# The low part of a group's first masked tile on GpSimd in layer 1's attention

## The chip, the cores and the metric

One core of one Trainium2 chip runs the kernel. The metric is the device time of one execution in microseconds; the number that counts is the median of the runs. The engines are TensorE (PE, with its weight loads as PEld), VectorE (DVE), ScalarE (ACT), GpSimd (POOL) and SyncE (SP), which issues the DMAs.

## The reference

Two layers of a backbone over 256 context tokens and 2048 latent tokens, 1024 wide. Layer 0 is latent attention beside a pooling branch. Layer 1, where the change lies, is windowed attention with grouped queries: 16 heads of 64, four groups of four heads that share a key head, blocks of 128 tokens, each reading its own block, its two neighbours within 128 tokens, and 256 cached context tokens, with a sink logit for each head.

```python
s_loc = jnp.einsum('bnqkgd,bnskd->bnkgqs', qb, kw).astype(jnp.float32) * scale
rel = kpos[:, None, :] - qpos[:, :, None]
valid = (jnp.abs(rel) <= SWA_WINDOW) & (kpos[:, None, :] >= 0) & (kpos[:, None, :] < T)
s_loc = jnp.where(valid[None, :, None, None], s_loc, NEG_INF)
s_ctx = jnp.einsum('bnqkgd,bpkd->bnkgqp', qb, ck).astype(jnp.float32) * scale
p = jax.nn.softmax(jnp.concatenate([s_loc, s_ctx, sk], axis=-1), axis=-1)
o = jnp.einsum('bnkgqs,bnskd->bnqkgd', p_loc, vw) + jnp.einsum('bnkgqp,bpkd->bnqkgd', p_ctx, cv)
```

A left neighbour's keys are masked along one diagonal and a right neighbour's along the other; the own block and the context are not masked.

## The kernel before

Everything is float32, and each product is made of high and low parts: a number is split into a part that PE reads in its short format (`fp32r`) and the rest. For a tile of probabilities that means the exponential (`pf`), its high part (`ph`) and the low part `pl = pf - ph`.

Layer 1's attention goes through 18 units of 128 queries (`UN1`, lines 1054 to 1058): two for the context tokens with two tiles of keys, and 16 for the latent ones. Each unit has four groups of heads (`g`), and each group goes through its tiles `i` of 128 keys by 4 x 128 queries. A unit inside has five: 0 the left neighbour (masked), 1 the own block, 2 the right neighbour (masked), 3 and 4 the context. The first latent unit has no left neighbour and the last no right one, so 15 units x 4 groups have a masked tile 0. In all there are 328 tiles (`seq1`).

Step `k` of the loop (lines 1288 to 1302) issues `scores1` of tile k, `low1` of tile k - 1, some look-ahead work (`approx1`: rough scores and their maximum, reduced by DVE in lines 1109 and 1115), and `pv1` of tile k - 3.

- `scores1`: two matmuls into one of three `S` banks (lines 1170, 1171). An unmasked tile gets its high part from ACT (line 1174). The exponential itself (line 1176) goes to one of two `bpf` buffers where the tile is masked or its low part is made by POOL, and back into its PSUM bank otherwise. A masked tile is then cut by POOL (line 1180).
- `low1`: a masked tile gets its high part now, by a copy on ACT, or on DVE in the last three units (line 1186). The low part is line 1188; `y1` says which engine makes it: POOL for tiles 1 and 3, DVE for the others.
- `pv1`: three matmuls into the bank `A` or `B` (lines 1200 to 1202); the third, line 1202, reads the low part. After the last tile of a group the sums are copied out and stored.

Every second unit `recip1` reads row sums back by DMA and adds them on DVE (line 1217). The output's weights and its first block of inputs (`mix_part`, lines 847, 848) are prepared in the same stretch. Instructions carry the waits that their tiles and buffers need. The order on each engine is not the code's: a planner (line 1409, `schedule_with_timeline_sim`) lays the program out by a clock of its own, puts on each engine what is ready by that clock, earlier code first, and hands out buffers as they come free by it.

Of the kernel before, what the change touches and what calls it, by code (L numbers as in the profile page):

```python
# [8 lines left out]
F32 = mybir.dt.float32  # L9
# [3 lines left out]
ALU = mybir.AluOpType  # L13
# [25 lines left out]
def hybrid_step(ctx: ExitStack, tc: tile.TileContext, I, O):  # L39
    nc = tc.nc  # L40
    pe, act, dve, pool, sp = nc.tensor, nc.scalar, nc.vector, nc.gpsimd, nc.sync

    def open_pool(name, side="left"):
        st = ExitStack()
        p = st.enter_context(tc.tile_pool(name=name, bufs=1, side=side, reuse_waits="tile"))
        return p, st.close
# [5 lines left out]
    def f(ap):  # L52
        return ap.bitcast(F32)
# [5 lines left out]
    def bank(tag, bufs):  # L59
        return psum.tile([128, 512], F32, tag=tag, name=tag, bufs=bufs)  # L60
# [988 lines left out]
    def key(kt):  # L1049
        if kt in (16, 17):  # L1050
            return ring["KAC"], ring["KBC"], VAC, VLC, kt - 16
        return KAR, KBR, VAR, ring["VLR"], kt - 12 if kt > 17 else kt % 8

    UN1 = [(128 * i, [(18, None), (19, None)]) for i in range(2)]
# [102 lines left out]

    LAG1, LATE = 3, NU1 - 3

    def y1(g, i):  # L1160
        return i in (1, 3)

    def scores1(u, g, i):
        bt = box["bt"]
        kt, mk = UN1[u][1][i]
        ka, kb, va, vl, t = key(kt)
        c = slice(128 * t, 128 * t + 128)
        qa, qb = [q[:, 4 * g:4 * g + 4] for q in QV[u % NQ]]
        S = bank("S", 3)
        pe.matmul(S, lhsT=ka[:, g, c], rhs=qa, start=True, stop=False)  # L1170
        pe.matmul(S, lhsT=kb[:, g, c], rhs=qb, start=False, stop=True)  # L1171
        ph = bt.tile([128, 512], F32R, tag="bph", name="bph", bufs=6)
        if mk is None:
            act.activation(out=ph, in_=S, func=AF.Exp, scale=SWA_SCALE)
        pf = S if mk is None and not y1(g, i) else bt.tile([128, 512], F32, tag="bpf", name="bpf", bufs=2)
        act.activation(out=pf, in_=S, func=AF.Exp, scale=SWA_SCALE)  # L1176
        if mk is not None:
            s = 1 - 2 * mk
            p4 = pf.rearrange("p (h n) -> p h n", h=4)
            pool.affine_select(out=p4, in_=p4, pattern=[[0, 4], [-s, 128]], base=0, channel_multiplier=s, compare_op=ALU.is_ge, fill=0.0)  # L1180
        live1[u, g, i] = (ph, pf)

    def low1(u, g, i):
        ph, pf = live1[u, g, i]
        if UN1[u][1][i][1] is not None:
            (dve.tensor_copy if u >= LATE else act.copy)(ph, pf)
        pl = box["bt"].tile([128, 512], F32R, tag="bpl", name="bpl", bufs=5)
        (pool if y1(g, i) else dve).tensor_tensor(out=pl, in0=pf, in1=f(ph), op=ALU.subtract)  # L1188
        live1[u, g, i] = (ph, pl)

    def pv1(u, g, i):
# [67 lines left out]
    bt, close_bt = open_pool("bt")  # L1259
# [28 lines left out]
    for k in range(-22, NST1 + LAG1 + 8):  # L1288
        now1[0] = k
        for fn in events1.pop(k, []):  # L1290
            fn()
        want = int(np.interp(k, *pace))
        q1_to(min(want // 8 + 2, sdone1[0] + NQ))
        if 0 <= k < NST1:
            scores1(*seq1[k])
            if k + 1 == NST1 or seq1[k + 1][0] != seq1[k][0]:
                sdone1[0] += 1
        if 1 <= k <= NST1:
            low1(*seq1[k - 1])
        look1_to(want)  # L1300
        if LAG1 <= k < NST1 + LAG1:
            pv1(*seq1[k - LAG1])
# [110 lines left out]
```

## Time and profile before

| what | us |
|---|---|
| median of three runs (lowest, highest) | 3175.36 (3166.04, 3183.04) |
| the profiled execution, its own time | 3180.69 |
| its span, first to last instruction | 3179.0 |
| layer 1's attention within the span | 2434 to 2945 |

In the page a busy share is that of the whole span, and a line number can be a helper's. The idle time that stands behind a group is put down to what ended it. Matmuls overlap: their shown length is longer than the step from one to the next. The times in the sections below are from the profiled execution.

### The profile page before, as it was taken

The numbers are of one execution on the slowest core, as the hardware profiler recorded it, in microseconds if no ns is written. First come the engines' busy times: TensorE is split into PE (matmuls) and PEld (weight loads), VectorE is DVE, ScalarE is ACT, GpSimd is POOL, SyncE is SP. The second block draws the span as 40 slices with busy tenths as digits, with TensorE's granted clock in tenths as the row PEclk, the third lists the DMA queues.
The fourth block names the chain that finished last, engine by engine and source line by source line (L and its number), as shares of the span: only waits on it lengthen the run. The fifth ranks groups of instructions, "written<-read, shape, count | busy, mean of one in ns | idle before, by whom it ended". The sixth has DMA issues, their size and how long they took to land.

```text
span 3179.0 us, 53411 instructions
## 1 busy us (share of the span) xinstructions
PE 3022.1 (95%) x19192; PEld 2596.5 (82%) x19192; DVE 2270.6 (71%) x4123; ACT 1776.8 (56%) x3579; POOL 1588.1 (50%) x1430
## 2 busy tenths in 40 slices
PE   6999998999999999999999999999997999999998
PEld 4999987897777777767789999999995776666997
DVE  6656757878898898888857556666325788787555
ACT  6444444436777777777774432323324777775432
POOL 3223242206877777877875435555001554545453
PEclk8999999999999999999999999999998999999999
DMA  6444468743202211221125463347436445541553
GB/s 237 146 142 140 143 203 251 236 129 89 55 18 57 61 45 31 52 73 37 54 64 176 153 198 126 120 127 209 131 103 132 87 101 102 112 88 47 164 172 113
DMA packets 380006, 375.31 MB, mean 118 GB/s; under 512 B 27796, under 2 KB 345276, under 8 KB 378588
## 3 DMA queue, kind: packets, MB, share of 16 engines
q1 hardware_dynamic: 379716, 371.90, 41.7%
q8 instruction: 150, 2.46, 0.3%
q14 instruction: 116, 0.95, 0.1%
q10 hardware_dynamic: 24, 0.01, 0.0%
HBM read 242.13 MB, written 129.24 MB: 117 GB/s over the span
## 4 chain that ended last, share of the span: by engine, by line
PE 59%; DVE 15%; DMA 11%; issue 5%; POOL 4%; ACT 4%; SPq 1%; DVEq 0%; POOLq 0%; ACTq 0%
PE S L113 9%; PE S L114 9%; PE S L115 9%; PE B L642 4%; PE M L553 4%; PE A L639 4%; PE M L114 3%; PE M L115 3%; PE M L113 3%; DVE pm L554 2%; PE S L1171 1%; PE S L1170 1%; DMA stg<-in_ada_w 1%; DVE xb L200 1%; DMA q_d<-ehl 1%
## 5 line engine op out<-in xcount | busy, mean ns | idle before, releaser
L629 POOL TENSOR_TENSOR acc<-acc,ph 128x512 f32<-128x512 f32 x352 | 459.6, 1306 | 58.6 <-ACT ph L605 43.8
L605 ACT ACTIVATE ph<-S 128x512 fp32r<-128x512 f32 (+1 forms) x592 | 350.4, 592 | 190.4 <-PE S L115 180.9
L554 DVE TENSOR_REDUCE pm<-M 128x1 f32<-128x512 f32 (+1 forms) x656 | 390.7, 625 | 36.3 <-PE M L553 32.8
L617 DVE TENSOR_TENSOR pl<-S,ph 128x512 fp32r<-128x512 f32 (+1 forms) x496 | 332.6, 676 | 65.7 <-ACT S L610 59.3
L113 PE MATMUL S<-hh,wh 128*128 128x256 f32 x1296 | 370.7, 287 | 5.8 <-ACT hh L199 3.0
L114 PE MATMUL S<-hl,wh 128*128 128x256 f32 x1296 | 369.6, 285 | 3.7 <-DVE hl L201 3.7
L115 PE MATMUL S<-hh,wl 128*128 128x256 f32 x1296 | 369.5, 285 | 2.5 <-POOL wl L57 2.5
L610 ACT ACTIVATE S<-S 128x512 f32<-128x512 f32 (+1 forms) x496 | 292.0, 589 | 0.0
L113 PEld LDWEIGHTS S<-hh,wh 128*128 128x128 f32 x1296 | 250.0, 193 | 10.0 <-ACT wh L56 3.3
L114 PEld LDWEIGHTS S<-hl,wh 128*128 128x128 f32 x1296 | 250.4, 193 | 6.0 <-DVE hl L201 4.3
L115 PEld LDWEIGHTS S<-hh,wl 128*128 128x128 f32 x1296 | 250.2, 193 | 4.3 <-POOL wl L57 2.9
L113 PE MATMUL S<-QS,KHL 97*128 97x512 f32 (+1 forms) x592 | 235.1, 397 | 2.5 <-DVE pl L617 2.0
L114 PE MATMUL S<-QS,KHL 97*128 97x512 f32 (+1 forms) x592 | 232.9, 393 | 0.0
L642 PE MATMUL B<-pl,VV 128*65 128x512 f32 (+1 forms) x592 | 230.6, 395 | 2.3 <-DVE pl L617 1.6
L115 PE MATMUL S<-QS,KHL 97*128 97x512 f32 (+1 forms) x592 | 232.0, 392 | 0.0
L553 PE MATMUL M<-KHL,QS 96*128 96x512 f32 (+1 forms) x656 | 219.5, 380 | 5.6 <-DVE pm L554 5.3
L639 PE MATMUL A<-ph,VV 128*128 128x512 f32 (+1 forms) x592 | 208.9, 396 | 0.7 <-ACT ph L605 0.7
L1188 POOL TENSOR_TENSOR bpl<-bpf,bph 128x512 fp32r<-128x512 f32 x136 | 178.3, 1311 | 58.8 <-ACT bpf L1176 42.9
L113 PE MATMUL M<-hh,oh 128*128 128x256 f32 x696 | 198.3, 285 | 4.0 <-ACT oh L56 4.0
L114 PE MATMUL M<-hl,oh 128*128 128x256 f32 x696 | 196.5, 282 | 0.0
L115 PE MATMUL M<-hh,ol 128*128 128x256 f32 x696 | 196.3, 282 | 0.0
L1180 POOL TENSOR_SCALAR_AFFINE_SELECT bpf<-bpf 128x512 f32<-128x512 f32 x120 | 77.1, 642 | 210.2 <-ACT bpf L1176 197.1
(387 smaller groups left out, 9636.6 us busy)
## 6 DMA issues: line engine op xcount, KB each, us to landing
q_d<-ehl SPq DMA_DIRECT2D x126, 256.0 KB
stg<-in_ada_w SPq DMA_DIRECT2D x48, 512.0 KB
xb<-in_xT SPq DMA_DIRECT2D x18, 1024.0 KB
xb<-x_d SPq DMA_DIRECT2D x18, 1024.0 KB
stg<-in_w SPq DMA_DIRECT2D x35, 512.0 KB
hh<-q_d SPq DMA_DIRECT2D x24, 512.0 KB
kn_d<-ehl SPq DMA_DIRECT2D x40, 256.0 KB
v_d<-ve SPq DMA_DIRECT2D x20, 512.0 KB
```

The costliest lines, as they stand in the source:

```text
L113: pe.matmul(ps, lhsT=wh, rhs=xh, start=i == 0, stop=False)
L114: pe.matmul(ps, lhsT=wh, rhs=xl, start=False, stop=False)
L115: pe.matmul(ps, lhsT=wl, rhs=xh, start=False, stop=i == n - 1)
L553: pe.matmul(ps[:, :w], lhsT=QS[u % 4][0:96, 0, 128 * s:128 * s + 128], rhs=KH[h % 2][0:96, c0:c0 + w], start=True, stop=True)
L554: dve.tensor_reduce(out=pms[u][:, s, i:i + 1], in_=ps[:, :w], axis=AX.X, op=ALU.max)
L605: act.activation(out=ph[:, :n], in_=S[:, :n], func=AF.Exp, scale=MLA_SCALE)
L610: act.activation(out=pf[:, :n], in_=S[:, :n], func=AF.Exp, scale=MLA_SCALE)
L617: (pool if i in YS else dve).tensor_tensor(out=pl[:, :n], in0=pf[:, :n], in1=f(ph)[:, :n], op=ALU.subtract)
L629: pool.tensor_tensor(out=acc[:, :n], in0=acc[:, :n] if ph0 is None else f(ph0)[:, :n], in1=f(ph)[:, :n], op=ALU.add)
L639: pe.matmul(A[:, :n], lhsT=V[:, kts[i], 0:128], rhs=ph[:, :n], start=i == 0, stop=i == nk - 1)
L642: pe.matmul(B[0:65, :n], lhsT=V[:, kts[i], 64:129], rhs=pl[:, :n], start=i == 0, stop=i == nk - 1)
L1188: (pool if y1(g, i) else dve).tensor_tensor(out=pl, in0=pf, in1=f(ph), op=ALU.subtract)
```

## The change

`y1` gets the unit in place of the group and is true for tile 0 too where that tile is masked. So in 60 groups (units 3 to 17, four groups each) the subtraction of tile 0 is issued to POOL, not DVE. `scores1` asks `y1` as well, but a masked tile had a `bpf` buffer already. Everything else stands.

```diff
-    def y1(g, i):
-        return i in (1, 3)
+    def y1(u, i):
+        return i in (1, 3) or i == 0 and UN1[u][1][0][1] is not None
...
-        pf = S if mk is None and not y1(g, i) else bt.tile([128, 512], F32, tag="bpf", name="bpf", bufs=2)
+        pf = S if mk is None and not y1(u, i) else bt.tile([128, 512], F32, tag="bpf", name="bpf", bufs=2)
...
-        (pool if y1(g, i) else dve).tensor_tensor(out=pl, in0=pf, in1=f(ph), op=ALU.subtract)
+        (pool if y1(u, i) else dve).tensor_tensor(out=pl, in0=pf, in1=f(ph), op=ALU.subtract)
```

## Rows read from the trace of the kernel before

**Rows 1.** The page's part 4: the chain that ended last, share of the span.

```profile
PE 59%; DVE 15%; DMA 11%; issue 5%; POOL 4%; ACT 4%; SPq 1%; DVEq 0%; POOLq 0%; ACTq 0%
```

**Rows 2.** Windows, layer 1's attention: length, then PE, PEld, DVE, ACT, POOL busy.

```profile
2434.00:2945.00 511.00, 478.69 (x2258) 340.86 (x2256) 401.10 (x920) 361.72 (x705) 252.89 (x257) 0.98 0.44 91
```

**Rows 3.** Waits, 2477 to 2942 us: who waited for whom, total us, times, longest.

```profile
ACT bpf L1176 <- DVE bpl L1188: 35.9, 36, 3.8
...
PEld A L1202 <- DVE bpl L1188: 14.5, 16, 3.9
...
PEld B L1202 <- DVE bpl L1188: 11.3, 16, 1.3
...
PE A L1202 <- DVE bpl L1188: 7.2, 8, 3.5
...
PE B L1202 <- DVE bpl L1188: 4.3, 8, 0.8
...
ACT bpf L1176 <- POOL bpl L1188: 3.4, 2, 3.0
```

**Rows 4.** Groups, 2434 to 2945 us: count, busy us, mean ns, idle before and releasers.

```profile
L1188 DVE TENSOR_TENSOR bpl<-bpf,bph 128x512 fp32r<-128x512 f32 x116 | 113.5, 978 | 16.9 <-ACT bph L1186 15.4
...
L1188 POOL TENSOR_TENSOR bpl<-bpf,bph 128x512 fp32r<-128x512 f32 x130 | 170.6, 1313 | 42.6 <-ACT bpf L1176 35.4 <-PE S L1171 2.9 <-ACT bph L1186 2.4
L1180 POOL TENSOR_SCALAR_AFFINE_SELECT bpf<-bpf 128x512 f32<-128x512 f32 x120 | 77.1, 642 | 210.2 <-ACT bpf L1176 197.1 <-PE M L1106 4.8 <-PE A L1201 3.0
```

**Rows 5.** Line 1188's DVE instructions: shortest, median, longest in ns, first and last start.

```profile
L1188 DVE TENSOR_TENSOR bpl<-bpf,bph x116: 675/742/1773, 2482.2 to 2936.8; 128x512 fp32r<-128x512 f32 x116
L1188 DVE TENSOR_TENSOR bpl<-S,bph x76: 628/680/692, 2409.1 to 2938.4; 128x512 fp32r<-128x512 f32 x76
```

**Rows 6.** Timeline of one group, engine by engine: start, length, idle before it.

```profile
2679.24 0.60 ACT L1176 ACTIVATE bpf<-S 128x512 f32<-128x512 f32 x1
...
2681.87 0.60 ACT L1176 ACTIVATE bpf<-S 128x512 f32<-128x512 f32 x1 [1.52 <-DVE bpl L1188]
...
2683.32 0.60 ACT L1176 ACTIVATE bpf<-S 128x512 f32<-128x512 f32 x1
2683.80 0.63 ACT L1186 CAST bph<-bpf 128x512 fp32r<-128x512 f32 x1
...
2680.38 1.40 DVE L1188 TENSOR_TENSOR bpl<-bpf,bph 128x512 fp32r<-128x512 f32 x1
...
2684.46 1.38 DVE L1188 TENSOR_TENSOR bpl<-bpf,bph 128x512 fp32r<-128x512 f32 x1 [0.95 <-ACT bph L1186]
...
2679.93 1.30 POOL L1188 TENSOR_TENSOR bpl<-bpf,bph 128x512 fp32r<-128x512 f32 x1 [0.35 <-ACT bpf L1176]
2682.55 0.64 POOL L1180 TENSOR_SCALAR_AFFINE_SELECT bpf<-bpf 128x512 f32<-128x512 f32 x1 [1.31 <-ACT bpf L1176]
2684.00 1.29 POOL L1188 TENSOR_TENSOR bpl<-bpf,bph 128x512 fp32r<-128x512 f32 x1 [0.82 <-ACT bpf L1176]
...
2682.74 0.39 PE L1202 MATMUL A<-bpl,VAR 128*65 128x512 f32 x1
2682.96 0.39 PE L1200 MATMUL A<-bph,VAR 128*65 128x512 f32 x1
...
2685.42 0.40 PE L1201 MATMUL A<-bph,VLR 128*64 128x512 f32 x1
2685.89 0.45 PE L1202 MATMUL A<-bpl,VAR 128*65 128x512 f32 x1
```

**Rows 7.** Timeline of DVE from 2516 us: a wait of `recip1` and what follows.

```profile
2519.13 0.19 DVE L1217 TENSOR_TENSOR rsum<-rsum 128x32 f32<-128x32 f32 x1 [2.87 <-DMA rsum<-o_d]
...
2521.60 0.69 DVE L1188 TENSOR_TENSOR bpl<-bpf,bph 128x512 fp32r<-128x512 f32 x1
```

**Rows 8.** Timeline of POOL and PE around the longest wait for a low part.

```profile
2773.11 2.50 POOL L847 TENSOR_TENSOR mg<-mg,mr 128x512 f32<-128x512 f32 x2 [2.24 <-issue]
...
2777.89 0.69 PE L1202 MATMUL A<-bpl,VAR 128*65 128x512 f32 x1 [3.49 <-DVE bpl L1188]
```

## The prediction

> **What bounds the kernel now.** I read the chain, the busy times of a stretch, the waits, and then groups and timelines of single places. The page's chain first: what ended last runs 59% through TensorE (PE) and 15% through VectorE (DVE) [rows 1]. Then the stretch of layer 1's attention, the only one that the change touches: 2434 to 2945 us, 511 us, with PE busy 478.7, DVE 401.1, ScalarE (ACT) 361.7 and GpSimd (POOL) 252.9 [rows 2]. So PE bounds it, and whatever the change does to DVE or POOL reaches the end only through PE's waits. These are 511 - 478.7 = 32.3 us of shown idle in all.
>
> The waits tell which of it has to do with the low parts. PE sat idle for a DVE low part (`bpl`, line 1188) for 7.2 + 4.3 = 11.5 us; its weight loader, which runs ahead of it, for 14.5 + 11.3 = 25.8 us in 32 waits [rows 3]. A 512-column matmul is shown 0.39 us long, but where nothing waits the next one starts 0.22 to 0.24 us after it [rows 6], so up to 0.16 us of each wait is drawn as busy: 11.5 + 32 x 0.16 = 16.6 us. That is the most that the change can give through these waits, 0.5% of the span. Put beside the loop's order (328 matmuls of line 1202, one a tile), the waits over 0.06 us are 11 before a group's first tile, 8.5 us together, with 3.5 of it in one [rows 8], and 17 before the third tile, 7.7 us, of which rows 6 end with one.
>
> **Why a third tile waits.** The masked and the POOL-made tiles of a group share two `bpf` buffers. In the group of [rows 6] exp of tile 1 ends at 2679.84; POOL makes its low part from 2679.93 to 2681.23; DVE starts tile 0's low part at 2680.38 and ends at 2681.78, 0.55 after POOL; 0.09 later ACT begins tile 2's exp, which had waited 1.52 us for that buffer. The same happens with tiles 3 and 2 (POOL 2684.00 to 2685.29, DVE to 2685.84), and PE's matmul stands at 2685.89 for it. ACT waits for a DVE low part 35.9 us in 36 waits, for a POOL one only 3.4 us in 2 [rows 3].
>
> DVE is slow here because it is held: its low parts out of SBUF take 675 ns at least, 742 in the middle and 1773 at most, those that read one operand from PSUM 680 in the middle and never over 692 [rows 5]. In rows 6 each held one ends just after POOL's. The Trainium skill says so as a rule (SBUF — State Buffer, Who interferes with whom): a VectorE instruction with two SBUF inputs and a GpSimd one that reads SBUF exclude each other, and the later one blocks fully. The trace agrees, by the 0.55 us between the two ends; a sum by the rule is the one that follows.
>
> **The change, part by part.**
> 1. Removed from DVE: 60 low parts (15 units x 4 groups whose first tile is masked). The 116 out of SBUF are these 60 and the 56 third tiles, mean 978 ns [rows 4]: 60 x 0.978 = 58.7 us of DVE's 401, of which 60 x (0.978 - 0.680) = 17.9 us is being held. DVE is not the bound; by itself this gives PE nothing, except where a first tile stood behind something else on DVE. Such a place: at 2519.13 DVE had idled 2.87 us for the DMA of `recip1`, and a first tile's low part was made only at 2521.60 [rows 7].
> 2. Added to POOL: 60 x 1.313 = 78.8 us [rows 4]. POOL goes from 252.9 to 331.7 of 511 us, 65%: not a bound by its sum. It idles 210 us before the masks, nearly all of it for ACT [rows 4]. No DMA is issued by the moved step, and no queue of SP is passed.
> 3. The order on POOL. The code issues tile 0's low part before tile 1's, but tile 1 is ready first: its exp ends at 2679.84, while the copy that tile 0's low part needs follows that exp on ACT, as the copy of tile 2 follows tile 3's exp at 2683.80 [rows 6]. The planner puts ready work first: POOL's mask of tile 2 is issued before tile 1's low part in the code and runs after it in rows 6. So: mask 0, low 1, low 0, mask 2, low 3. Low 0 then ends at 2681.23 + 1.29 = 2682.52, not 2681.78: 0.74 us later.
> 4. What that does to PE. The matmul of low 0 stood at 2682.74 [rows 6], so here it still finds it ready. Where it stood right behind DVE's end it is 0.7 us later. I count four first tiles whose matmul already waited by over 0.3 us with POOL's tile 1 just ahead (units 4, 8, 10, 12): 4 x 0.74 = 3.0 us lost, and in the last two units, where PE has no look-ahead matmuls to fill with, some 2 us more.
> 5. What it does to the buffers. The planner gives a buffer to the first tile that needs one after it came free; that low 1 can be that one is seen in the two waits of ACT for POOL [rows 3]. Now it is always low 1, free at 2681.23. Tile 2's exp starts at 2681.28, not 2681.87; mask 2 waits for low 0 until 2682.52, as it stood before (2682.55); tile 3's exp takes the other buffer at 2682.8, not 2683.32; low 3 runs 2683.45 to 2684.75, not 2684.00 to 2685.29; low 2 on DVE, held as now, ends at 2685.30, not 2685.84; and the matmul that stood at 2685.89 (0.47 us after its neighbour, so 0.24 late) finds it. The next group may start half a microsecond sooner, against waits of 0.1 to 1 us. Of the third tiles' 7.7 us I take 6 as gone.
> 6. First tiles' own 8.5 us. In the 3.5 us one POOL itself was late: two multiplications of 2.50 us for the output's first block stood ahead of tile 1's low part [rows 8]. That one stays. Of the other 5.0 some 2 stand in the groups of point 4; the 3 behind other DVE work I take as gone, and 2 us more in places like rows 7, where the look-ahead's reductions stood in the same queue.
>
> Behind the moved step on POOL stand mask 2 and low 3; for them wait ACT's copy (DVE's in the last three units), DVE's low 2 and PE's matmul: point 5 has their times.
>
> Sum: -6 - 3 - 2 + 3 + 2 = -6 us. Bounds: all of the waits gone, -16.6; nothing gone and the losses of 4 doubled, +10. What is late next: DVE's low part of tile 2, still held by POOL, and PE itself.
>
> The profiled execution took 3180.69 us, a span of 3179.0 and 1.7 around it; -6 on it is 3174.7. The median of the runs is 3175.36 (3166.04 to 3183.04), and the forecast is for a median: 3175.4 - 6 = 3169 us.
>
> **The rivals.**
> A. *No net change*, 3175 us. PE is 94% busy in the stretch; what the third tiles win the first ones lose. The Trainium skill has a sentence for it (Perfetto Trace Analysis, Optimizing Scalar/DVE Operations): the two engines share a read port, so moving work between them "might not help". Rows 5 speak for it, the 0.74 us against 0.59 us in the group above too; against it that PE has its slack at the first tile.
> B. *Slower, by POOL's queue.* It decides at which buffer the planner gives tile 2. If that stays tile 0's, or if low 0 goes ahead of low 1 and the planner holds the rest behind it, tile 2's exp starts at 2682.57, 0.7 us later than before, mask 2 and low 3 behind it, and PE, with 0.38 us between the third tile's low part and its matmul on the mean of the 56, loses about 0.74 - 0.38 = 0.36 us in each of 56 groups: +20 us, 3195 us. For it: six steps in a row on one engine. Against it: the two waits for POOL in rows 3, and that tile 1 is ready first in nearly all groups.
> C. *Much faster.* All 16.6 us of waits go, and with DVE freed its look-ahead reductions come sooner: 3158 us.
> D. *It doesn't reach the chip as written.* The planner moves other work by its own clock; a first tile whose mask came early might leave the order untouched and DVE's freed time be spent waiting. In time this is A.
>
> **How the numbers follow.** Forecast 0.48, A with D 0.32, B 0.10, C 0.10. A measurement of this kernel tells about 0.5% (16 us) from no change. Faster by more needs nearly all of C, or the forecast with 10 us more: 0.10. Slower by more is most of B: 0.08. Same: 0.82. The range takes in the forecast, A, the bounds -16.6 and +10, and leaves out most of B: 3156 to 3186 us.
>
> **What would show it.** On POOL 196 low parts of about 1.3 us, 60 more; on DVE 56 out of SBUF, still held, 76 out of PSUM unchanged at 680 ns. ACT's wait for a DVE low part falls from 35.9 us to below 12, and one for POOL's rises. PE's waits for DVE's low parts fall by half or more, and new ones for POOL's come, of 3 to 6 us. The forecast is wrong if ACT's tile 2 waits for tile 0's low part (B), if PE's waits for POOL's low parts are over 10 us (A or B), or if the stretch outside layer 1's attention moves by more than a few microseconds.

## The result, and the profile after

The changed kernel takes 3268.0 us (median; 3267.23 to 3271.03) against 3176.02 before in the same comparison (3166.04 to 3183.04): a ratio of 1.0286, with an interval of 1.0269 to 1.0303. It is 92 us slower; the forecast was 3169 us in a range of 3156 to 3186. The profiled execution took 3267.23 us with a span of 3265.5, so 86.5 us of span are to be found.

First the place. Windows of units 3 to 15, from the first score matmul of unit 3 to that of unit 16: length, then busy time of PE, PEld, DVE, ACT and POOL with instructions, mean granted clock of PE, share and rate of the DMAs. The kernel before:

```profile
2477.50:2883.60 406.10, 389.93 (x1841) 279.33 (x1840) 338.20 (x795) 305.77 (x595) 206.00 (x213) 0.99 0.47 96
```

The kernel after, the same 13 units, then the rest of the attention:

```profile
2482.20:2976.60 494.40, 422.71 (x1861) 290.72 (x1860) 299.85 (x746) 315.95 (x599) 273.67 (x266) 0.93 0.39 79
2976.60:3034.60 58.00, 54.28 (x261) 37.48 (x260) 28.69 (x41) 33.25 (x62) 43.04 (x40) 1.00 0.20 55
```

494.4 - 406.1 = 88.3 us: the whole loss lies in these 13 units, in which the change lies too. It is not in DVE (38 us less busy) nor in POOL (busy 55% of the stretch). PE's idle time, by length less busy, rose from 16.2 to 71.7 us, and its mean granted clock fell from 0.99 to 0.93. As the clock has two levels here, 0.50 and 1.00, a mean of 0.93 says that 0.07 x 2 of 494.4 us, some 69 us, went by at the lower one (1.2 GHz), against some 8 us before.

The waits name what PE stood for (2480 to 3035 us: who waited for whom, total us, times, longest); the rows answer to [rows 3]:

```profile
POOL bpl L1188 <- ACT bph L1186: 46.1, 48, 2.4
...
ACT bpf L1176 <- POOL bpl L1188: 31.9, 52, 3.1
...
PE M L1106 <- DMA hh<-q_d: 27.2, 7, 5.2
...
PE M L1106 <- DMA mix0h<-q_d: 14.8, 4, 5.1
...
ACT bpf L1176 <- DVE bpl L1188: 11.7, 14, 2.2
...
PE M L1132 <- DVE bmm L1125: 8.3, 11, 1.1
...
PE A L1202 <- DVE bpl L1188: 5.0, 8, 2.2
PE B L1202 <- POOL bpl L1188: 4.8, 8, 0.7
PE A L1200 <- ACT bph L1186: 4.8, 3, 3.8
...
PE B L1202 <- DVE bpl L1188: 3.7, 5, 0.9
...
PE A L1202 <- POOL bpl L1188: 1.6, 3, 0.7
...
PE B L1200 <- ACT bph L1186: 1.3, 5, 0.3
```

The low parts are a small matter: 8.7 us for DVE's and 6.4 for POOL's, 15.1 together against 11.5 before [rows 3]. The large rows are lines that the change does not touch: the look-ahead's first matmuls (line 1106) stand for the DMA of their queries (`hh` and `mix0h`, read from `q_d`), 42.0 us in 11 waits, one in each of units 5 to 15. The kernel before has one such wait, in unit 15:

```profile
PE M L1106 <- DMA hh<-q_d: 2.1, 1, 2.1
```

This is one of the 11, in unit 8 (timeline, SP's DMA issues and PE; start, length, idle before):

```profile
2659.81 0.60 SPq L1084 DMA_DIRECT2D mix0h<-q_d  x1
...
2661.14 0.58 SPq L1085 DMA_DIRECT2D mix0h<-q_d  x1
...
2664.21 0.39 PE L1201 MATMUL B<-bph,VLC 128*64 128x512 f32 x1
2668.19 1.19 PE L1106 MATMUL M<-KAR,mix0h 128*128 128x128 f32 x4 [3.59 <-DMA mix0h<-q_d]
...
2670.46 0.63 PE L1201 MATMUL B<-bph,VLC 128*64 128x512 f32 x1
2670.88 0.63 PE L1170 MATMUL S<-hh,KAR 128*128 128x512 f32 x1
2671.31 0.63 PE L1171 MATMUL S<-hl,KBR 96*128 96x512 f32 x1
...
2677.61 0.40 PE L1200 MATMUL A<-bph,VAR 128*65 128x512 f32 x1
2677.85 0.40 PE L1201 MATMUL A<-bph,VLR 128*64 128x512 f32 x1
```

and the windows of the wait, of the time behind it and of the time after that:

```profile
2664.50:2668.20 3.70, 0.11 (x2) 0.04 (x1) 0.00 (x0) 0.92 (x2) 2.97 (x3) 0.78 1.22 212
2668.20:2673.00 4.80, 4.80 (x14) 3.73 (x15) 1.65 (x5) 0.58 (x1) 0.04 (x1) 0.50 0.33 48
2673.50:2678.00 4.50, 4.50 (x28) 3.77 (x27) 3.52 (x12) 3.36 (x7) 1.89 (x2) 1.00 0.18 41
```

The load of unit 10's queries is issued at unit 8's start, because the three buffers of queries are used in turn and this one came free only with unit 7's last scores (unit 10 takes unit 7's buffer). The look-ahead on these queries is the next thing in PE's order; it starts 7.05 us after the second DMA's issue, having waited 3.59. Then 512-column matmuls start every 0.43 us at a granted clock of 0.50, and from 2673.5 on every 0.23 to 0.24. In the kernel before, at the start of its unit 9, such a load is issued and first read so:

```profile
2659.88 0.59 SPq L1084 DMA_DIRECT2D hh<-q_d  x1
2660.51 0.67 SPq L1085 DMA_DIRECT2D hh<-q_d  x1
...
2672.07 0.45 PE L1106 MATMUL M<-KAR,hh 128*128 128x384 f32 x1
```

There is other work in between, and nothing waits.

What moved is therefore PE's order, which the planner writes. I count by how much the look-ahead is ahead: the units of it that stand before a unit's first score matmul on PE, less the units already scored (the **lead**; 1.0 means that the unit about to start has its maxima and no more, 2.0 that the next one has them too). Before, it is 1.12 at unit 3, 1.38 to 1.88 at units 4 to 14, and 2.0 first at unit 15, the one unit with a wait for queries. After, it is 1.12 at unit 3, 1.5 at unit 4 and 2.0 from unit 5 on, where the waits begin. 2.0 is the point at which the next look-ahead needs the queries whose load has only just become possible.

The balance for units 3 to 15, with the waits taken from this stretch alone: 42.0 - 2.1 = 40 us of waits for queries; 2 us more for low parts (11.9 against 9.5 before), 8 for the maxima (8.3 against 0.5), 6 for ACT's copies of line 1186 (4.8 + 1.3, none before). Then the half clock. Part of its 69 us went by within the waits, where nothing is lost: the granted clock is 0.78 in the window of the wait above and 0.67 to 0.87 in seven of the 11, some 13 us at the lower level in all. That leaves 69 - 13 - 8 = 48 us more of work at half speed than before, some 24 us lost. Together 80 of 88.3 us; the other 8 are not accounted for (PE has 20 matmuls more in this stretch, 1861 against 1841).

### The profile page after: what moved, and what is told of

It reads as the page before. It is cut to its first block, busy times and chain, and to the rows that moved or that the text cites. A ratio compares the mean times of both kernels' runs of the same rounds, so it can differ in the third digit from the quotient of the medians.

```text
span 3265.5 us, 53434 instructions
## 1 busy us (share of the span) xinstructions
PE 3057.1 (94%) x19192; PEld 2606.2 (80%) x19192; DVE 2228.2 (68%) x4063; ACT 1788.3 (55%) x3579; POOL 1667.7 (51%) x1490
## 4 chain that ended last, share of the span: by engine, by line
PE 58%; DVE 15%; DMA 12%; issue 5%; POOL 5%; ACT 4%; SPq 1%; DVEq 0%; POOLq 0%; ACTq 0%
PE S L114 8%; PE S L113 8%; PE S L115 8%; PE M L553 3%; PE B L642 3%; PE A L639 3%; PE M L114 3%; PE M L115 3%; PE M L113 3%; DMA hh<-q_d 2%; DVE pm L554 2%; PE S L1170 1%; DVE pl L617 1%; PE S L1171 1%; DVE xb L200 1%
## 5 line engine op out<-in xcount | busy, mean ns | idle before, releaser
L1188 POOL TENSOR_TENSOR bpl<-bpf,bph 128x512 fp32r<-128x512 f32 x196 | 251.8, 1298 | 93.3 <-ACT bph L1186 48.4
L1109 DVE CUSTOM_DVE_ANT_0 junk<-M,band 128x384 bf16<-128x384 f32 (+1 forms) x256 | 132.5, 535 | 110.2 <-PE M L1106 107.8
```

The lines of the kernel that those rows point to most:

```text
L1188: (pool if y1(u, i) else dve).tensor_tensor(out=pl, in0=pf, in1=f(ph), op=ALU.subtract)
```

## The experiments

Two theories go through the expectations. **T1**: the loss is the look-ahead's place in PE's order (each wait for the queries, and the half clock behind it); the 60 moved low parts cost or give next to nothing by themselves. **T2**: the loss is the moved work itself, six steps in a row on POOL for each group (rival B of the prediction), and the look-ahead only drifts because of it. A kernel whose name begins with a is the changed one with an edit, with b the one before with the same edit. Ratios are against the kernel before, run beside each.

**The edge.** The first edit makes the look-ahead's instructions wait, in the planner's order, for the last score matmul issued ahead of them in the code. The lead is then 1.0 in both kernels:

```diff
-            approx1(u, g, hp)
+            if box.get("last") is None:
+                approx1(u, g, hp)
+            else:
+                with tc.issue_after(box["last"]):
+                    approx1(u, g, hp)
...
-        pe.matmul(S, lhsT=kb[:, g, c], rhs=qb, start=False, stop=True)
+        box["last"] = pe.matmul(S, lhsT=kb[:, g, c], rhs=qb, start=False, stop=True).ins
```

`a_pin`, the changed kernel with the edge:

> The changed kernel, with one edge more: on TensorE each look-ahead step is queued behind the second score matmul that the code issues just before it, so the planner can't pull it forward; in the built order the look-ahead then stands 1.0 units ahead throughout (2.0 in the changed kernel, 1.1 to 1.9 in the kernel before). Theory 1 (the look-ahead was pulled forward until it stood right behind the load of its queries; TensorE waits for that DMA once a unit, and its clock falls after): no more waits of over 2 us for that load, 3165 to 3190 us. Theory 2 (GpSimd's longer chain itself costs 1.5 us for each of the 60 moved tiles): 3240 to 3270 us.

Measured: 3258.4 us, 1.0244 (1.0215 to 1.0272).

`b_pin`, the kernel before with the edge:

> The kernel before with the same edge, as a control: what the edge itself does. Both theories: 3165 to 3190 us; a difference between this and the changed kernel with the edge is what the moved low parts cost or give when the order of the look-ahead is the same.

Measured: 3285.7 us, 1.0324 (1.0292 to 1.0355). T1's numbers for both were missed: the waits for queries are gone, but another took their place. At a lead of 1.0 a unit's maxima are ready only as it starts, and they have to go through a DMA (`bms`, line 1135) into the rows that the second score matmul reads. In `b_pin` (line numbers 4 higher), around unit 9's start:

```profile
2711.61 0.25 ACT L1134 COPY bms<-M 32x128 f32<-32x128 f32 x1
...
2713.74 1.86 SPq L1135 DMA_DIRECT2D hl<-bms  x1
...
2722.12 0.76 PE L1175 MATMUL S<-hl,KBR 96*128 96x512 f32 x1 [5.92 <-DMA hl<-bms]
```

and its sums of waits:

```profile
PE S L1175 <- DMA hl<-bms: 44.8, 9, 6.3
PE S L1175 <- DMA mix0l<-bms: 17.2, 5, 5.6
```

In `a_pin` the two rows say 28.6 us in 9 and 7.9 in 3. So the look-ahead has a late input on either side: too early and it stands for its queries, too late and the scores stand for its result. Both give one wait of 2 to 6 us in most units, and most such units take 34 to 40 us, where before most take 29 to 33. T2 is hurt too: with the same edge the kernel with the moved low parts is the faster one, by 27 us. At this lead the moved work is not without worth, then: the maxima are what is late, and they come sooner. From the end of a unit's last look-ahead matmul (line 1114) to the issue of its maxima's DMA went 5.1 to 6.8 us in `a_pin` and 7.0 to 7.9 us in `b_pin`, with 11.2 once (units 4 to 16), and the waits for `bms` are 36.5 us against 62.0. Which of the steps between, on DVE, ACT and SP, gave this was not tested.

`a_u6`, only the 16 low parts of units 3 to 6 moved:

```diff
-        return i in (1, 3) or i == 0 and UN1[u][1][0][1] is not None
+        return i in (1, 3) or i == 0 and u < 7 and UN1[u][1][0][1] is not None
```

> Only the first 16 of the 60 tiles are moved (units 3 to 6), the rest stays on VectorE. In the built order the look-ahead still climbs to 2.0 units ahead at unit 5 and stays there to the end. Theory 1: nearly the whole loss stays, 3235 to 3270 us, with a wait for the queries in each unit to 15, though those units are as before. Theory 2: 16 x 1.5 = 24 us, about 3200 us.

Measured: 3227.7 us, 1.0139 (1.0105 to 1.0173), between the two. Units 3 to 6 took 140.6 us (122.0 before); units 8 to 15, in which nothing is moved, took 273.6 (254.9 before). In those the lead stayed at 2.0 and PE waited once a unit, in all but unit 11, for `q_d`, 0.9 to 3.3 us. So 19 us of loss stand in units with the work as before, which T2 can't give; that the waits are shorter there, T1 as I had put it does not say.

`a_bpf3`, the change with a third `bpf` buffer:

```diff
-        pf = S if mk is None and not y1(u, i) else bt.tile([128, 512], F32, tag="bpf", name="bpf", bufs=2)
+        pf = S if mk is None and not y1(u, i) else bt.tile([128, 512], F32, tag="bpf", name="bpf", bufs=3)
```

> The changed kernel with three buffers for the exponentials (bpf) in place of two. In the built order the look-ahead stands 1.1 to 1.5 units ahead. Theory 1: 3160 to 3185 us, no wait of over 2 us for the queries. Theory 2: the chain on GpSimd is as long, though a third buffer relieves it: 3200 to 3260 us.

Measured: 3181.2 us, 1.0002 (0.9988 to 1.0016). The whole loss is gone. With the third buffer the planner wrote an order with a lead of 1.12 to 1.5 (units 3 to 15), no wait of PE for `q_d` is left, and the clock is at its upper level nearly throughout (units 3 to 15):

```profile
2483.70:2880.10 396.40, 384.07 (x1819) 275.20 (x1818) 305.64 (x715) 300.56 (x593) 270.15 (x264) 1.00 0.49 98
```

These are 9.7 us less than in the kernel before, which units 16 and the time ahead of unit 3 use up again (38.8 us for unit 16 against 34.7, and unit 3 starts 6.2 later). This run alone doesn't tell T1 from T2, since the buffer takes away the waits on POOL as well as changing the order.

**The same order in both kernels.** To take the planner out, a second edge, beside the first, makes each score matmul wait for the look-ahead's last matmul issued ahead of it, so that scores and look-ahead stand on PE in the code's order; the number of steps by which the code issues the look-ahead ahead sets the lead (8, 15 and 20 below):

```diff
-            pe.matmul(ps[:, 256 * i:256 * i + 256], lhsT=qa[:, h0 + i], rhs=ka, start=i == 0, stop=i == 1)
+            box["ahead"] = pe.matmul(ps[:, 256 * i:256 * i + 256], lhsT=qa[:, h0 + i], rhs=ka, start=i == 0, stop=i == 1).ins
...
-        want = int(np.interp(k, *pace))
+        want = min(int(np.interp(k + 8, *pace)), 8 * (sdone1[0] + NQ))
...
-            scores1(*seq1[k])
+            with tc.issue_after(box["ahead"]):
+                scores1(*seq1[k])
```

`a_mid2`, the changed kernel, 8 steps, lead 1.5:

> As a_mid1, and the scores can't pass the look-ahead either: both stand on TensorE in the code's order, 1.5 units ahead. It has b_mid2 as its partner, with the same order of scores and look-ahead and the 60 tiles on VectorE. Theory 1: within 1% of b_mid2, either way, both under 3215 us. Theory 2: 60 to 90 us above b_mid2.

Measured: 3217.2 us, 1.013 (1.0108 to 1.0153).

`b_mid2`, the kernel before, 8 steps, lead 1.5:

> The kernel before with the order of a_mid2, 1.5 units ahead. Theory 1: 3170 to 3215 us, with no wait of over 2 us once a unit. Theory 2: the same.

Measured: 3221.5 us, 1.0134 (1.0108 to 1.0161). Both lie a little over the 3215 us that T1 set as their limit. A fixed order costs both some 40 to 44 us, so it is no remedy; but within it, with the scores and the look-ahead in the same order on PE, the 60 moved low parts are worth -4 us, with intervals of 7 us either way: nothing that can be told. What the change was meant to touch did move, ACT's wait for a DVE low part (line 1180 here), in `b_mid2` and then in `a_mid2`:

```profile
ACT bpf L1180 <- DVE bpl L1192: 70.8, 62, 3.1
...
ACT bpf L1180 <- DVE bpl L1192: 5.5, 7, 1.6
```

The time shows nothing of it.

`b_lead`, the kernel before, 15 steps, lead 1.88:

> The kernel before, no tile moved, with both orders fixed as in b_mid2 and the pace 15 steps earlier in place of 8: the look-ahead stands 1.9 units ahead, just behind the load of its queries, nearly as in the changed kernel. Theory 1: the loss comes without any moved tile: a wait of 3 to 5 us for the queries in each unit from 3 to 15 and half the clock behind it, 50 to 90 us above b_mid2. Theory 2: as b_mid2 within 15 us.

Measured: 3222.3 us, 1.0144 (1.0121 to 1.0166); the loss that T1 foretold did not come. In this order the look-ahead on new queries begins some 8 us into a unit. Unit 8:

```profile
2660.12 0.60 SPq L1084 DMA_DIRECT2D mix0h<-q_d  x1
2660.78 0.66 SPq L1085 DMA_DIRECT2D mix0h<-q_d  x1
...
2668.60 0.47 PE L1106 MATMUL M<-KAR,mix0h 128*128 128x128 f32 x2
```

7.82 us after the second issue nothing is left to wait for. The lead as such costs nothing; what T1 needs is that PE comes to the look-ahead before the queries have landed, in the 7 to 8 us behind the second issue.

`b_lead20`, the kernel before, 20 steps, lead 2.0:

> The kernel before, no tile moved, both orders fixed as in b_mid2 and b_lead, the pace 20 steps earlier: the look-ahead of a unit now begins at the very step at which its queries are loaded, 2.0 units ahead as in the changed kernel. In b_lead (1.9) it began 8 us later and no wait for the queries came. Theory 1, sharpened (what costs is a first user right behind its DMA, not the lead as such): a wait of 2.5 to 5 us for the queries in each unit and 3 to 7 us of half clock behind it, 40 to 80 us above b_mid2's 3221. Rival (the wait and the clock are hidden by other work, and the moved tiles make the loss): within 15 us of b_mid2.

Measured: 3290.3 us, 1.0353 (1.033 to 1.0375), 69 us over `b_mid2` with no low part moved. Its waits are those of the changed kernel:

```profile
PE M L1106 <- DMA hh<-q_d: 24.6, 8, 4.3
PE M L1106 <- DMA mix0h<-q_d: 13.7, 4, 4.3
```

and so are its clock and its time in the window of units 3 to 15:

```profile
2498.00:2994.60 496.60, 431.26 (x1814) 292.98 (x1813) 349.74 (x756) 306.64 (x593) 206.84 (x213) 0.92 0.39 78
```

`b_mid2`, the same window:

```profile
2488.70:2922.50 433.80, 394.10 (x1814) 268.56 (x1813) 338.07 (x756) 303.37 (x593) 209.30 (x213) 0.99 0.44 90
```

The same number of instructions on every engine, and 62.8 us more in these 13 units; PE's idle time differs by 25.6 us, and the clock of 0.92 against 0.99 stands for the rest. This shows T1's mechanism without the change.

**Other leads.** Three more kernels have the first edge alone with an earlier look-ahead.

`a_mid1`, the changed kernel, 8 steps, lead 1.5:

> The changed kernel with the edge of a_pin (look-ahead not ahead of the code's scores) and the pace 8 steps earlier: in the built order the look-ahead stands 1.5 units ahead, between a_pin's 1.0, where the scores waited for the DMA of the maxima, and the changed kernel's 2.0, where the look-ahead waits for the queries. Theory 1 (a DMA that lands just behind its first user, once a unit, and the clock after it, make the loss; the moved tiles themselves cost next to nothing): no such wait on either side, 3165 to 3190 us. Theory 2 (the moved tiles cost 1.5 us each in whatever order): over 3240 us.

Measured: 3202.5 us, 1.0067 (1.0039 to 1.0094). In units 3 to 15 PE waits neither for `q_d` nor for `bms`, as T1 said, but the time is 12 us over its range; `b_mid1`, next, comes out alike without the moved work, so it is put down to the edge and the pace.

`b_mid1`, the kernel before with the same edit; its lead came out at 1.0 to 1.5 (with one wait of 3.0 us for `bms` left):

> The kernel before with the edge and the pace of a_mid1: its partner, no tile moved. In the built order the planner puts the look-ahead 1.0 to 1.5 units ahead, not 1.5 throughout. Theory 1: 3175 to 3215 us, within 1% of a_mid1 (3203).

Measured: 3197.5 us, 1.0064 (1.0044 to 1.0084). Five microseconds apart, within their intervals, though the two orders are alike and not the same: again the moved low parts are worth nothing that can be told.

`a_p12`, the changed kernel, 12 steps, lead 1.75:

> As a_mid1 (1.5 units ahead, 3203 us) with the pace 12 steps earlier in place of 8: 1.75 units ahead, as the kernel before has it in its middle, with all 60 tiles moved. Theory 1, sharpened: still no wait for the queries of over 1 us in most units, 3185 to 3215 us; the loss comes only at 2.0. Rival (the loss grows with the lead): some 3235 us, halfway to the changed kernel.

Measured: 3200.9 us, 1.007 (1.0051 to 1.0089). From the changed kernel's 3268.0 an edge that only holds the look-ahead back to a lead of 1.5 or 1.75 takes off 66 us; neither has a wait for `q_d`.

`b_bpf3`, the kernel before with three `bpf` buffers:

> The kernel before with three bpf buffers: the partner of a_bpf3 (3181 us), no tile moved. In the built order the look-ahead stands 1.0 to 1.1 units ahead. If the moved tiles cost or give little by themselves: 3165 to 3200 us. If 1.0 is too late for the maxima's DMA as in a_pin, up to 3260 us with waits for that DMA.

Measured: 3211.0 us, 1.0092 (1.0067 to 1.0117): a buffer more makes it slower. The planner wrote an order with a lead of 1.0 and 1.12 in turn, and the waits are those of `b_pin`, in six units:

```profile
PE S L1171 <- DMA hl<-bms: 18.4, 4, 4.9
PE S L1171 <- DMA mix0l<-bms: 8.8, 2, 4.5
```

So an edit that removes waits lost 1% by the order it brought about, as the change itself did; and of the 30 us between `a_bpf3` and `b_bpf3` these waits are 27, while `a_bpf3` has none for `bms` in units 3 to 15. Their orders differ, so the pair does not say what the low parts are worth.

No kernel here was faster than the one before by more than its interval.

## Why the prediction was wrong

It forecast 3169 us; the time was 3268.0. By its own steps:

- **1 and 2, the moved work: right.** POOL has 196 low parts, 251.8 us in all, 1298 ns each (1313 was taken); DVE keeps 56 out of SBUF and 76 out of PSUM at 683 ns. The rows of line 1188 after, against [rows 5]:

```profile
L1188 POOL TENSOR_TENSOR bpl<-bpf,bph x196: 1259/1288/1767, 2413.5 to 3029.9; 128x512 fp32r<-128x512 f32 x196
...
L1188 DVE TENSOR_TENSOR bpl<-S,bph x76: 627/683/692, 2414.7 to 3028.4; 128x512 fp32r<-128x512 f32 x76
L1188 DVE TENSOR_TENSOR bpl<-bpf,bph x56: 677/687/1758, 2491.0 to 3008.8; 128x512 fp32r<-128x512 f32 x56
```

- **The hold on DVE: right.** In the next fence DVE's low part starts 0.56 us after POOL's, takes 1.28 us and ends 0.55 after it, the same 0.55 as before [rows 6]. The rule of the Trainium skill that the prediction named for it (SBUF — State Buffer, Who interferes with whom) agrees with this row too.

- **3, the order on POOL: wrong.** It was to be mask 0, low 1, low 0, mask 2, low 3. A group at 2699 us, after:

```profile
2700.14 1.29 POOL L1188 TENSOR_TENSOR bpl<-bpf,bph 128x512 fp32r<-128x512 f32 x1
2700.70 1.28 DVE L1188 TENSOR_TENSOR bpl<-bpf,bph 128x512 fp32r<-128x512 f32 x1 [5.89 <-ACT bph L1186]
...
2702.06 1.08 ACT L1176 ACTIVATE bpf<-S 128x512 f32<-128x512 f32 x2
...
2702.72 0.63 POOL L1180 TENSOR_SCALAR_AFFINE_SELECT bpf<-bpf 128x512 f32<-128x512 f32 x1 [1.29 <-ACT bpf L1176]
2703.39 0.62 ACT L1186 CAST bph<-bpf 128x512 fp32r<-128x512 f32 x1 [0.25 <-POOL bpf L1180]
2704.09 2.48 POOL L1188 TENSOR_TENSOR bpl<-bpf,bph 128x512 fp32r<-128x512 f32 x2 [0.73 <-ACT bph L1186]
```

  The exponentials of tiles 0 and 1 end at 2703.14. After the mask of tile 0 POOL could make low 1, but it stands 0.73 us for ACT's copy and then makes low 0 and low 1 one behind the other; 48 such waits make 46.1 us. Low 0 goes first, as in the code. The step took "ready first by the trace" for "first by the planner's clock", and these are two clocks.

- **4 to 6, the waits for low parts: half right.** ACT's wait for a DVE low part fell from 35.9 to 11.7 us (below 12 was forecast) and the one for POOL rose from 3.4 to 31.9, by the order of step 3 (a rise was forecast, with no size). PE's wait for DVE's fell from 11.5 to 8.7, not by half; POOL's came in at 6.4 (3 to 6 forecast). Their sum is +4 us against the forecast -6, inside the bound of +10. The pairs at a lead near 1.5 say the same of the net worth of the moved work, -4 and +5 us. That was rival A, *no net change*, and the sentence of the Trainium skill beside it ("might not help"; Perfetto Trace Analysis, Optimizing Scalar/DVE Operations) agrees with these pairs. At a lead of 1.0, where the maxima are late, the kernel with the move was 27 us the faster.

- **What failed** is a term that the prediction put at nothing without a reason: what the planner does with the work that the change does not touch. Rival D names it and says "In time this is A"; the sum has no term for it, and every step priced the change against PE's order of before. In its place the runs showed 88.3 us in units 3 to 15: some 40 us of waits for queries and 24 us of half clock, behind a look-ahead at a lead of 2.0. Held back to 1.5 or 1.75 the changed kernel gives 66 us back (`a_mid1`, `a_p12`), and at 2.0 the kernel before loses 69 us without the change (`b_lead20` against `b_mid2`). The prediction knew that the order is a planner's and asked what it would do on POOL and with the buffers; it did not ask what it would do with the look-ahead on PE, the one stream with slack in both directions and a DMA on either side. The rows to ask from were there: the wait of 2.1 us for `hh` in unit 15 of before is the price of being too early, 2.1 us and a half clock behind it, in a unit of 34.4 us where the two ahead of it take 30.6 and 29.7. Some 4 to 5 us a unit over 11 units, by these lengths, would have been a rival at about +50 us; the range ended at +11.

- **The rivals.** B had the sign, 3195 us, and one of its conditions came true (low 0 ahead of low 1). Of ACT's 52 waits for POOL, put beside the loop's order (328 exponentials of line 1176, one a tile), 17 stand before a third tile, 14.3 us together, and 29 before a fourth, 15.5 us; so the sign that the prediction set for B, ACT's tile 2 waiting for tile 0's low part, showed too. But its price of 0.36 us a group on PE is not what was lost: PE's waits for low parts rose by 4 us, not 20. The other sign, set for A or B, over 10 us of PE's waits for POOL's low parts, did not show. C did not come. D was closest to the truth in kind, "the planner moves other work by its own clock", but it was priced at nothing and given no chance of its own.

What stays open is why the planner puts the look-ahead forward when the low part of tile 0 goes to POOL. That its clock sees PE idle behind a longer chain on POOL and fills the gap with the look-ahead would fit the third buffer, which shortens that chain and gave a lead of 1.12 to 1.5, and `a_u6`, where 16 moved tiles were enough and the lead stayed afterwards. It was only argued; the planner's clock is in no trace.

## What to carry to other kernels

Where a planner writes the order, price an edit against the order that it will write, and look first for the stream that can slide: what bounds it on the early side, what on the late side, and what one wait at either end costs. Compare an edit with its undoing under one fixed order before anything is said of its own worth, and name that order: at a lead near 1.5 the worth is -4 to +5 us, beside 92 us for the change with the order that it brought about, and at a lead of 1.0 it is -27. A once-a-unit wait of 3 to 5 us for a DMA on the bounding engine costs more here than its length, for the clock: some 24 us beside 40 us of waits in the changed kernel.

## What the runs showed of the hardware

The clock was the unexpected part. Behind a wait of 3.59 us PE worked at a granted clock of 0.50, the 1.2 GHz level, from 2668.2 to 2673.0, and 512-column matmuls started every 0.43 us in place of 0.23; in units 3 to 15 that came to some 69 us at the lower level, 56 of them outside the waits, or 28 us of lost work, 0.9% of the span. The wait's length alone did not decide it: behind 2.3 us in unit 5 and 3.3 us in unit 13 of the changed kernel the clock stayed at its upper level (2.4 GHz), while in `a_u6` it fell behind 2.0 us. The Trainium skill (TensorE: Matmul & The Clock Gate, Part 1: The HAM clock gate) puts the penalty of the clock's ramp below 1% of a typical kernel's span, and says that it differs from run to run of one kernel. The 0.9% here, from these 13 units alone, lies just under that figure, as the clock fell in most of them; the rows just named differ likewise, from unit to unit.

A load of queries (`q_d`, 512 KB a DMA as the page's issues have it) kept PE waiting until 7.05 us after the second DMA's issue in unit 8 of the changed kernel, and until 7.05 to 8.04 us in the 11 units. What differs between a wait and none is how soon PE comes to it: 3.46 us after that issue in unit 8 (7.05 less the wait of 3.59), 7.82 us in `b_lead`. Some 4 us of other work in between make the difference.
